# Another order and other gaps for the steps of a chunk recurrence inside a dense matmul stream

## The chip, the cores and the metric

One core of a Trainium2 chip runs one inference step of a two-layer streaming encoder. The metric is device time in microseconds (us); the median of three runs of the kernel before is 3050.2 us (3047.46 to 3052.67). Engines are named as in the profile: PE (TensorE matmuls), PEld (its weight loads), DVE (VectorE), ACT (ScalarE), POOL (GpSimd) and SP (SyncE, whose queue issues the DMAs).

## The reference

Layer one is an RWKV-7 time mixing over 1024 prompt frames and 64 frames of a running stream, then a SwiGLU feed-forward; layer two is sliding-window attention with a shared K/V, then another feed-forward. What matters here is the recurrence, for each of 16 heads with a 64 by 64 state:

```python
def step(s, inp):
    r_t, w_t, k_t, v_t, a_t, b_t = inp
    sa = jnp.einsum('bhvk,bhk->bhv', s, a_t)
    s = s * w_t[:, :, None, :] + sa[..., None] * b_t[:, :, None, :] + v_t[..., None] * k_t[:, :, None, :]
    return s, jnp.einsum('bhvk,bhk->bhv', s, r_t)
```

The feed-forward, which runs beside it, is `(silu(x @ w_gate) * (x @ w_up)) @ w_out` with 2816 hidden units on 1024 features.

## The kernel before, in words

**The recurrence in chunks.** The frames are cut into 17 chunks of 64 (16 of the prompt, one of the running stream). Within a chunk the steps are replaced by matrix products and by the inverse of a 64 by 64 triangular matrix for each head. Chunks 0 to 7 run in one way (`recur_free`), chunks 8 to 16 in another (`recur`), beside the feed-forward of the first half of the prompt ("half A"). Only `recur` is touched by the change.

**The steps of one chunk**, each a Python generator whose `yield`s separate pieces; a piece holds PE work and the DVE, ACT and POOL work that hangs on it:

- `prep` loads r, k, a, s and scales them (elementwise on DVE, ACT, POOL); then the *norms* (16 small matmuls into `p_rp`, read by DVE L187); then two *triangle groups* (8 row pairs of 64x128 matmuls each into `p_rp`, masked into the tile `r_G` by DVE L210); then the *bonus* (one 128x512 product into `p_rp`, DVE L219).
- `inverse16` first works on DVE alone. ACT copies the diagonal blocks out of `r_G` (four copies, L325), DVE transposes them (L330), eliminates (L334 to L359: among them seven pairs of L348 and L351) and turns the result back (L363 to L369). Four *joins* follow, groups of small matmuls into `p_rc`, each of which needs what DVE or ACT made of the join before it: join 1 needs the tile `r_ixd` that DVE L369 wrote; join 2 needs ACT L385; join 3 needs DVE L392 and a second L369; join 4 needs ACT L403 and DVE L404, which copy the result of join 3 out of PSUM. DVE L415 and ACT L414 then write the finished inverse `W`.
- `chain` is the serial part, five pieces: c0 (X times the state, copied out by ACT L435), c1 (times `W`, copied out by DVE L440 and ACT L441 into `r_sv`), c2 (the new state, DVE L447 and L448), c3 and c4 (the output `p_ry`; a one-element POOL memset, L459, stands between its two halves as an ordering point).
- `turned` (called "keys" in `recur`) transposes `r_BK` on PE; `post` normalises the output and, one round later, transposes it.

**A round.** The main loop of `recur` interleaves the chain of chunk i with the joins of chunk i+1 and with `prep` of chunk i+2, and ends by starting the DVE part of the inverse of chunk i+2.

**What sets the order.** From chunk 8 on, PE's order is written by hand. The dense code emits its matmuls in threes of 512 columns (`Dense.mm`, lines L604 to L606: high by high, low by high, high by low part), and after each three it calls `Pump.tick`, which subtracts 0.44 ns per column plus 6 ns from a need. When the need is used up, the pump takes the next piece of `recur`, whose PE instructions are then put at this place of the stream. So a `yield x * us` in `recur` says how much dense matmul time is put on PE before the next piece: a three counts 0.68 us of it. The recurrence's own matmuls are not counted. `FREE` holds the scale, 1.5, and an unscaled gap at the end of a round. PE runs its stream in order: a piece whose inputs are late holds up the dense matmuls behind it. The order on DVE, ACT, POOL and SP is made by the scheduler from priorities and its own estimate of times; there, too, each engine runs in order.

`turns` is the part in which triangle groups (`g`) and joins (`v`) take turns:

```python
for gap in (1.2, 1.4, 1.2, 1.4):
    for x in (g, v):
        if x and next(x, x) is not x:
            yield gap * scale * us
```

The last `next` of `g` ends the generator, and an ended one yields no gap; the order before is therefore triangle 0, join 1, triangle 1, join 2, bonus, join 3, join 4.

Of the kernel before, what the change touches and what calls it, by code (L numbers as in the profile page):

```python
# [499 lines left out]


LOW = 2.5
FREE = (1.5, 5.0)
D, T_P, T_S, NCH = 1024, 1024, 64, 17
NF = 22
RMS_EPS = 1e-5
# [239 lines left out]
def tile_stream_step(ctx: ExitStack, tc: tile.TileContext, I, O):  # L746
# [485 lines left out]
    def recur(chunks, M, base, low, scale, free, ends):  # L1232


        def step(g, p):
            rw.two.at(p, p)
            next(g)
        us = 1000.0
        inv, fill = low + 0.05, low + 0.2
        chunks, ds, gs, vs = list(chunks), [{} for _ in chunks], {}, {}  # L1240

        def load(i, p):
            gs[i] = rw.prep(chunks[i], ds[i])
            step(gs[i], p)

        def inverse(i, p):
            vs[i] = rw.inverse16(ds[i])
            step(vs[i], p)

        def keys(i, p):  # L1250
            rw.two.at(p, p)
            rw.turned(ds[i])

        def turns(g, v, p):

            for gap in (1.2, 1.4, 1.2, 1.4):
                for x in (g, v):
                    if x and next(x, x) is not x:
                        yield gap * scale * us
        load(0, base)  # L1260
        yield 16 * us
        step(gs[0], base)
        yield 4 * us
        rw.two.at(inv, inv)
        yield from turns(gs[0], None, base)
        inverse(0, base)
        keys(0, base)
        load(1, inv)
        yield 12 * us
        step(gs[1], inv)  # L1270
        yield 4 * us
        rw.two.at(inv, inv)
        yield from turns(gs[1], vs[0], inv)
        inverse(1, inv)
        old = None
        for i, ch in enumerate(chunks):
            g, v = None, vs.get(i + 1)
            k = rw.chain(ch, ds[i], M)
            step(k, base)
            yield 1.8 * scale * us  # L1280
            step(k, base)
            if old:
                step(old, fill)
            yield 1.8 * scale * us
            step(k, base)
            M = ds[i]["M"]
            if i + 1 < len(chunks):
                yield scale * us
                keys(i + 1, inv)
            if i + 2 < len(chunks):  # L1290
                load(i + 2, inv)
                g = gs[i + 2]
            yield 2 * scale * us
            step(k, base)
            yield 1.6 * scale * us
            step(k, base)
            if ch in ends:
                M = ends[ch](M)
            old = rw.post(ch, ds[i])
            step(old, fill)  # L1300
            yield 2 * scale * us
            if g:
                step(g, inv)
                yield 2 * scale * us
            rw.two.at(inv, inv)
            yield from turns(g, v, inv)
            if i + 2 < len(chunks):
                inverse(i + 2, inv)
            yield free * us
        step(old, fill)  # L1310
# [12 lines left out]
    def saved(M):  # L1323
# [3 lines left out]
        return M  # L1327

    pump.start(recur(range(8, 17), M, 3, 4, *FREE, {
        15: saved, 16: lambda M: nc.sync.dma_start(O["wkv_s"], M.rearrange("p a b -> p (a b)"))}), 3)  # L1330
    prio(4)
# [361 lines left out]
```

## Time and profile before

| | |
|---|---|
| median of 3 runs | 3050.2 us |
| the profiled execution: its time | 3049.59 us |
| its span, first to last instruction | 3047.8 us |
| PE busy | 2849.6 us (93%) |
| DVE, ACT, POOL busy | 1828.2 (60%), 1342.9 (44%), 911.8 us (30%) |
| mean granted PE clock | 0.96 of full speed |
| `recur` and the dense work beside it | about 700 to 1290 us of the span |

In a row of a group or of the timeline, "L404 DVE COPY r_ixd<-p_rc 32x256" is line 404, its engine, its operation, the tile that it writes and those that it reads (buffer numbers left out); "[2.77 <-DVE r_ixd L404]" says that the engine stood idle for 2.77 us just before, and that the last thing it waited for was that instruction. Idle time counts only on an engine whose order sets the end.

### The profile page before, as it was taken

To read this page: it belongs to the slowest core of one execution; us is meant where nothing else is said; L and a number is where in the kernel's file an instruction comes from. 1 tells how busy PE (TensorE), PEld (TensorE's weight loads), DVE (VectorE), ACT (ScalarE), POOL (GpSimd) and SP (SyncE) were. 2 spreads that over 40 slices of the span, in tenths; PEclk is the share of its full clock that TensorE was granted. 3 is DMA by queue.
4 is the path that set the end of the run, shared out by engine and by line. 5 is a ranking of instruction groups with operands and counts; after the bars stand their busy time and mean duration, and the time that the engine had idled before them with its cause. 6 is when DMAs were issued, how large, how long until landed. Compare 5 with 4: busy or idle time off the path is not lost. (4 is left out here: it accounts for less than half of the span.)

```text
span 3047.8 us, 53525 instructions
## 1 busy us (share of the span) xinstructions
PE 2849.6 (93%) x20802; PEld 2455.3 (81%) x20802; DVE 1828.2 (60%) x3630; ACT 1342.9 (44%) x2485; POOL 911.8 (30%) x795
## 2 busy tenths in 40 slices
PE   6898888978899999999999999999999999999998
PEld 5677677876677777787789999888777888999998
DVE  8887789967777676457654333565554345533334
ACT  7766665544444444334653222344554233322222
POOL 6554134333333333324211222143111222322221
PEclk9999878988999999999999999999999999999999
DMA  4645353344233222352212222222222332322222
GB/s 145 173 121 151 112 139 93 108 121 124 67 94 107 92 84 84 105 143 81 68 49 70 84 81 81 79 82 83 63 67 75 95 93 73 104 84 84 84 84 70
DMA packets 262055, 289.23 MB, mean 95 GB/s; under 512 B 125029, under 2 KB 143973, under 8 KB 261801
## 3 DMA queue, kind: packets, MB, share of 16 engines
q1 hardware_dynamic: 261800, 285.81, 31.6%
q8 instruction: 163, 2.67, 0.4%
q14 instruction: 92, 0.75, 0.1%
HBM read 243.18 MB, written 41.16 MB: 93 GB/s over the span
## 5 line engine op out<-in xcount | busy, mean ns | idle before, releaser
L604 PE MATMUL dp<-xh,wh 128*128 128x288 f32 (+2 forms) x3480 | 1194.8, 344 | 34.6 <-ACT xh L596 15.1
L605 PE MATMUL dp<-xl,wh 128*128 128x288 f32 (+2 forms) x3480 | 1173.4, 337 | 6.7 <-DVE xl L597 5.1
L606 PE MATMUL dp<-xh,wl 128*128 128x288 f32 (+2 forms) x3480 | 1168.5, 336 | 0.0
L564 ACT CAST wh<-wr 128x512 fp32r<-128x512 f32 x730 | 447.0, 619 | 843.5 <-PE dp L605 672.9
L604 PEld LDWEIGHTS dp<-xh,wh 128*128 128x128 f32 x3480 | 669.0, 193 | 115.9 <-ACT xh L596 18.1
L605 PEld LDWEIGHTS dp<-xl,wh 128*128 128x128 f32 x3480 | 669.8, 192 | 69.8 <-DVE xl L597 9.0
L606 PEld LDWEIGHTS dp<-xh,wl 128*128 128x128 f32 x3480 | 669.6, 192 | 57.6 <-issue 2.8
L565 POOL TENSOR_TENSOR wl<-wr,wh 128x512 fp32r<-128x512 f32 x243 | 333.5, 1372 | 1055.1 <-ACT wh L564 965.0
L565 DVE TENSOR_TENSOR wl<-wr,wh 128x512 fp32r<-128x512 f32 x487 | 380.0, 783 | 418.5 <-ACT wh L564 412.3
L604 PE MATMUL dp<-mh,wh 128*128 128x288 f32 (+1 forms) x808 | 255.0, 316 | 4.3 <-DVE hx L1135 2.6
L606 PE MATMUL dp<-mh,wl 128*128 128x288 f32 (+1 forms) x808 | 254.5, 315 | 0.0
L605 PE MATMUL dp<-ml,wh 128*128 128x288 f32 (+1 forms) x808 | 254.0, 314 | 0.0
L1135 DVE TENSOR_TENSOR a_xB<-dp,a_xB 128x288 f32<-128x288 f32 x352 | 158.2, 456 | 85.0 <-PE dp L606 84.6
L1116 DVE TENSOR_TENSOR st<-st,dp 128x288 f32<-128x288 f32 (+1 forms) x132 | 70.2, 532 | 220.9 <-PE dp L606 220.5
L1118 POOL TENSOR_TENSOR xl<-st,xh 128x288 fp32r<-128x288 f32 (+1 forms) x102 | 100.5, 985 | 316.1 <-ACT xh L1117 307.3
L604 PEld LDWEIGHTS dp<-mh,wh 128*128 128x128 f32 x808 | 152.7, 189 | 14.8 <-DVE hx L1135 3.6
L606 PEld LDWEIGHTS dp<-mh,wl 128*128 128x128 f32 x808 | 152.5, 189 | 8.7 <-issue 2.4
L605 PEld LDWEIGHTS dp<-ml,wh 128*128 128x128 f32 x808 | 152.7, 189 | 7.0 <-issue 1.1
L1135 DVE TENSOR_TENSOR hx<-dp,hx 128x512 f32<-128x512 f32 x176 | 119.8, 685 | 45.3 <-PE dp L606 44.1
L1114 ACT ACTIVATE st<-dp 128x288 f32<-128x288 f32 (+1 forms) x132 | 62.1, 470 | 92.5 <-PE dp L606 92.1
L1117 ACT CAST xh<-st 128x288 fp32r<-128x288 f32 (+1 forms) x102 | 50.2, 492 | 110.0 <-DVE st L1116 109.0
L597 POOL TENSOR_TENSOR xl<-st,xh 128x512 fp32r<-128x512 f32 (+2 forms) x37 | 64.7, 1759 | 70.2 <-ACT xh L596 66.2
(378 smaller groups left out, 3839.6 us busy)
## 6 DMA issues: line engine op xcount, KB each, us to landing
wr<-in_ffn_in SPq DMA_DIRECT2D x352, 256.0 KB
wr<-in_ffn_out SPq DMA_DIRECT2D x176, 256.0 KB
wr<-in_rkv SPq DMA_DIRECT2D x90, 256.0 KB
wr<-in_rwo SPq DMA_DIRECT2D x32, 256.0 KB
wr<-in_wq SPq DMA_DIRECT2D x32, 256.0 KB
wr<-in_wo SPq DMA_DIRECT2D x32, 256.0 KB
r_r_s<-s_s SPq DMA_DIRECT2D x17, 256.0 KB
r_sv<-s_vt SPq DMA_DIRECT2D x17, 256.0 KB
```

The lines of the kernel that those rows point to most:

```text
L564: nc.scalar.copy(h, x)
L565: (nc.gpsimd if self.turn % 3 == 0 else nc.vector).tensor_tensor(out=l, in0=x, in1=h, op=ALU.subtract)
L597: (eng or self.nc.vector).tensor_tensor(out=lo, in0=x, in1=hi, op=ALU.subtract)
L604: self.nc.tensor.matmul(ps, lhsT=wh, rhs=xh, start=i == 0, stop=False)
L605: self.nc.tensor.matmul(ps, lhsT=wh, rhs=xl, start=False, stop=False)
L606: self.nc.tensor.matmul(ps, lhsT=wl, rhs=xh, start=False, stop=i == last)
L1114: S.activation(t[o], p, AF.Silu)
L1116: V.tensor_tensor(out=t[o], in0=t[o], in1=p, op=ALU.mult)
L1117: S.copy(a.hi[:, q], t[o])
L1118: G.tensor_tensor(out=a.lo[:, q], in0=t[o], in1=a.hi[:, q], op=ALU.subtract)
L1135: V.tensor_tensor(out=self.x[m][:, q], in0=p, in1=self.x[m][:, q], op=ALU.add)
```

## The change

It changes nothing that is computed and moves only gaps and pieces in `recur`:

- `turns` lists its pieces: join 1, triangle 0, join 2, triangle 1, join 3, bonus, join 4, with gaps of 1.6, 1.6, 1.2, 2.0, 1.6, 3.0 and 0.6 us (times 1.5) behind them. Each join now comes ahead of the piece of `prep` with which it is paired, and the bonus with the longest gap stands between join 3 and join 4.
- In the main loop the gap ahead of c4 grows from 1.6 to 2.4, the two behind `post` and behind the norms shrink from 2 to 1.
- The gap at the end of a round shrinks from 5.0 to 3.0 us (unscaled).

```diff
-FREE = (1.5, 5.0)
+FREE = (1.5, 3.0)
...
         def turns(g, v, p):
 
-            for gap in (1.2, 1.4, 1.2, 1.4):
-                for x in (g, v):
-                    if x and next(x, x) is not x:
-                        yield gap * scale * us
+            for x, gap in ((v, 1.6), (g, 1.6), (v, 1.2), (g, 2.0), (v, 1.6), (g, 3.0), (v, 0.6), (g, 0.0)):
+                if x and next(x, x) is not x:
+                    yield gap * scale * us
...
             yield 2 * scale * us
             step(k, base)
-            yield 1.6 * scale * us
+            yield 2.4 * scale * us
             step(k, base)
             if ch in ends:
                 M = ends[ch](M)
             old = rw.post(ch, ds[i])
             step(old, fill)
-            yield 2 * scale * us
+            yield scale * us
             if g:
                 step(g, inv)
-                yield 2 * scale * us
+                yield scale * us
             rw.two.at(inv, inv)
             yield from turns(g, v, inv)
             if i + 2 < len(chunks):
                 inverse(i + 2, inv)
             yield free * us
```

How the change moves instructions is shown at two places on DVE, in the round around 950 us of the trace before (the one that quoted rows of the timeline come from; `r_f_531` is the work tile of the inverse that starts there, `r_ixd` and `p_rc` the tiles of the joins of the chunk before it). The first place is where DVE copies the result of join 3. Before:

```order
L330 STREAM_TRANSPOSE r_f_531_10217<-r_f_529_10210 128x512
L334 SCALAR_TENSOR_TENSOR r_f_531_10217<-r_f_531_10217,lanes 128x16x16
L343 TENSOR_TENSOR r_f_532_10221<-xl,r_nl_9937 128x128
L335 TENSOR_TENSOR r_f_531_10217<-r_f_531_10217,r_nl_9937 128x16x16
L219 TENSOR_TENSOR r_vf_10126<-p_rp_10128,r_vf_10126 128x512
L168 SCALAR_TENSOR_TENSOR r_rkr_10436<-r_r_a_10417,vecs 128x512
L340 TENSOR_TENSOR r_f_532_10221<-r_f_531_10217 128x128
L169 SCALAR_TENSOR_TENSOR r_rkr_10436<-r_rkr_10436,r_r_k_10416 128x512
L341 TENSOR_TENSOR r_f_531_10217<-r_f_531_10217,r_f_532_10221 128x8x16
L406 COPY r_G_9320<-r_AR_9159 64x8x64
L343 TENSOR_TENSOR r_f_532_10221<-xl,r_nl_9937 128x128
L404 COPY r_ixd_9599<-p_rc_10137 32x256
```

The change:

```order
L394 TENSOR_SCALAR W<-r_ixd_9677,lanes 128x8x32
L210 TENSOR_TENSOR r_G_10067<-p_rp_10150,c_mask 128x512
L210 TENSOR_TENSOR r_G_10067<-p_rp_10151,c_mask 128x512
L565 TENSOR_TENSOR wl_10369<-wr_10370,wh_10368 128x512
L330 STREAM_TRANSPOSE r_f_531_10295<-r_f_529_10288 128x512
L1116 TENSOR_TENSOR st_10089<-st_10089,dp_10103 128x512
L406 COPY r_G_9420<-r_AR_9210 64x8x64
L334 SCALAR_TENSOR_TENSOR r_f_531_10295<-r_f_531_10295,lanes 128x16x16
L343 TENSOR_TENSOR r_f_532_10299<-xl,r_nl_9997 128x128
L404 COPY r_ixd_9677<-p_rc_10177 32x256
```

The copy L404 moved ahead of L335, L219, L168, L340, L169, L341 and the second L343, and the second triangle group's masking (L210) now stands between join 2 (L394) and it.

The second place is where DVE copies the result of c1, in the round two later (around 1090 us). Before:

```order
L367 STREAM_TRANSPOSE r_f_622_11501<-r_f_622_11501 128x256
L368 COPY r_ixd_11525<-r_f_622_11501 128x256
L369 STREAM_TRANSPOSE r_ixd_11525<-r_ixd_11525 128x256
L1116 TENSOR_TENSOR st_11529<-st_11529,dp_11543 128x512
L172 TENSOR_TENSOR r_r_a_11715<-r_r_a_11715,r_rt_11721 128x512
L565 TENSOR_TENSOR wl_11791<-wr_11792,wh_11790 128x512
L1135 TENSOR_TENSOR hx_7492<-dp_11606,hx_7492 128x512
L440 COPY r_sv_11565<-p_rc_11618 64x8x64
```

The change:

```order
L172 TENSOR_TENSOR r_r_a_11776<-r_r_a_11776,r_rt_11782 128x512
L363 TENSOR_SCALAR r_f_622_11586<-r_f_622_11586,lanes 128x8x16
L1135 TENSOR_TENSOR hx_7534<-dp_11666,hx_7534 128x512
L367 STREAM_TRANSPOSE r_f_622_11586<-r_f_622_11586 128x256
L565 TENSOR_TENSOR wl_11905<-wr_11906,wh_11904 128x512
L1135 TENSOR_TENSOR hx_7541<-dp_11674,hx_7541 128x512
L565 TENSOR_TENSOR wl_11911<-wr_11912,wh_11910 128x512
L368 COPY r_ixd_11610<-r_f_622_11586 128x256
L440 COPY r_sv_11642<-p_rc_11681 64x8x64
L496 TENSOR_TENSOR r_g_11253<-p_ry_11185,r_g_11253 128x512
```

L440 still stands behind nearly the whole elimination of the next inverse; in this round the last turn (L369) has moved behind it, and two more rows of dense work (L1135, L565) stand ahead of it.

## The prediction

> **What bounds the kernel now.** I read the page first, then the stretches of time, then PE's idle time by group, then the timeline of one round.
>
> ```profile
> span 3047.8 us, 53525 instructions
> PE 2849.6 (93%) x20802; PEld 2455.3 (81%) x20802; DVE 1828.2 (60%) x3630; ACT 1342.9 (44%) x2485; POOL 911.8 (30%) x795
> ```
>
> PE is the bound. The stretches say where it is not full (columns: stretch, its length, busy us and count of PE, PEld, DVE, ACT, POOL, granted PE clock, DMA share, GB/s):
>
> ```profile
> 665.00:1305.00 640.00, 579.46 (x5488) 448.22 (x5487) 424.29 (x837) 257.32 (x401) 205.09 (x177) 0.94 0.33 99
> 800.00:1212.00 412.00, 382.23 (x3962) 296.69 (x3963) 288.54 (x598) 171.06 (x263) 133.01 (x119) 0.95 0.29 89
> 1700.00:1800.00 100.00, 99.81 (x752) 99.33 (x751) 34.53 (x64) 28.00 (x55) 22.29 (x21) 1.00 0.26 84
> ```
>
> Dense work alone keeps PE at 99.81 of 100 us and full clock. Beside the recurrence PE loses 29.8 of 412 us to waiting and 5% of its clock. A microsecond won on PE there is won at the end, since PE is full afterwards and DMA at about 0.3. What the recurrence's matmuls wait for, over 665 to 1305 us:
>
> ```profile
> L109 PE MATMUL p_rc<-r_ixd 32*32 32x16 f32 (+1 forms) x864 | 16.6, 192 | 25.1 <-DVE r_ixd L404 23.9 <-ACT r_ixd L403 1.1
> L109 PE MATMUL p_ry<-r_M,r_AR 64*64 64x64 f32 x288 | 12.3, 224 | 8.1 <-POOL r_by L459 8.1
> L109 PE MATMUL p_rp<-r_AR,r_BK 64*128 64x128 f32 x288 | 22.5, 295 | 3.2 <-DVE r_n L187 3.2
> ```
>
> So join 4 costs 25.0 us waiting for the copies of join 3 (eight rounds, about 3 each), and the second half of c3/c4 costs 8.1 us behind POOL's memset. One round on PE (step, and how it is fed):
>
> ```profile
> 940.67 1.16 PE L109 MATMUL p_rp<-r_AR,r_BK 64*128 64x128 f32 x16
> 944.05 0.72 PE L109 MATMUL p_rc<-r_ixd 32*32 32x16 f32 x64
> 946.91 1.02 PE L109 MATMUL p_rp<-r_rkr,c_bd 128*128 128x512 f32 x2
> 949.25 0.21 PE L109 MATMUL p_rc<-r_ixd,r_G 32*32 32x32 f32 x1
> 952.16 0.24 PE L109 MATMUL p_rc<-r_ixd 32*32 32x32 f32 x2
> 955.17 1.06 PE L109 MATMUL p_rc<-r_ixd 32*32 32x32 f32 x30 [2.77 <-DVE r_ixd L404]
> 965.76 1.15 PE L109 MATMUL p_rc<-r_sv,r_G 128*64 128x64 f32 x32
> 969.81 1.15 PE L109 MATMUL p_rc<-r_rt,W 64*64 64x64 f32 x32
> 974.25 1.19 PE L109 MATMUL p_rc<-r_sv,r_BT 128*64 128x64 f32 x32
> ```
>
> These are triangle 1, join 2, bonus, join 3, join 4 (its first two matmuls, then the rest 3.0 us later), c0, c1, c2. DVE in the same round, from the start of the next inverse to the copy for join 4:
>
> ```profile
> 948.22 0.71 DVE L330 STREAM_TRANSPOSE r_f<-r_f 128x512 f32<-128x512 f32 x1 [0.62 <-ACT r_f L325]
> ...
> 950.66 0.41 DVE L335 TENSOR_TENSOR r_f<-r_f,r_nl 128x256 f32<-128x256 f32 x1
> 951.00 0.68 DVE L219 TENSOR_TENSOR r_vf<-p_rp,r_vf 128x512 f32<-128x512 f32 x1
> 951.60 0.68 DVE L168 SCALAR_TENSOR_TENSOR r_rkr<-r_r_a,vecs 128x512 f32<-128x512 f32 x1
> 952.20 1.13 DVE L340 TENSOR_TENSOR r_f<-r_f 128x128 f32<-128x128 f32 x1
> 953.25 0.68 DVE L169 SCALAR_TENSOR_TENSOR r_rkr<-r_rkr,r_r_k 128x512 f32<-128x512 f32 x1
> ...
> 954.69 0.43 DVE L404 COPY r_ixd<-p_rc 32x256 f32<-32x256 f32 x1
> ```
>
> Join 3 ended near 950, but its copy L404 came at 954.69: DVE was not idle but busy with other work that stands ahead of it.
>
> The half clock comes from the same stall. Dense matmuls start 0.42 us apart just behind a join 4, 0.24 a little later:
>
> ```profile
> 895.22 1.05 PE L109 MATMUL p_rc<-r_ixd 32*32 32x32 f32 x30 [4.21 <-DVE r_ixd L404]
> ...
> 897.23 0.63 PE L606 MATMUL dp<-xh,wl 128*128 128x512 f32 x1
> 897.65 0.63 PE L604 MATMUL dp<-xh,wh 128*128 128x512 f32 x1
> ...
> 900.16 0.39 PE L604 MATMUL dp<-xh,wh 128*128 128x512 f32 x1
> 900.40 0.39 PE L605 MATMUL dp<-xl,wh 128*128 128x512 f32 x1
> ```
>
> **The change part by part.** It adds and removes no work; outside the recurrence every engine's order is as before. The gaps of a round sum to 12.2 x 1.5 + 9.0 x 1.5 + 5.0 = 36.8 us before and 11.0 x 1.5 + 11.6 x 1.5 + 3.0 = 36.9 after, so the same dense work passes in a round, and all that can change is waiting.
>
> *Join 4.* A dense matmul takes 0.233 us start to start. From triangle 1 to join 4 the change has 42 dense matmuls (9.8 us) and three steps that each add a little: triangle 1 and 9 matmuls took 944.05 - 940.67 = 3.38, so 1.3; join 3 and 9 took 2.91, so 0.8; the bonus and 6 took 2.34, so 0.9. Join 4 is reached 12.8 us after triangle 1. DVE starts L330 7.5 us after triangle 1 here (948.22 - 940.67), as it waits for ACT's four copies, and less in other rounds; one round earlier triangle 1 was at 879.33:
>
> ```profile
> 885.72 0.71 DVE L330 STREAM_TRANSPOSE r_f<-r_f 128x512 f32<-128x512 f32 x1 [2.92 <-ACT r_f L325]
> ```
>
> That is 6.4; I take 6.7. From L330 to the end of L404 the order now has 2.3 to 4.2 us of work, without the 4 us of L335, L219, L168, L340, L169 and its neighbours. L404 ends 9.0 to 10.9 us after triangle 1: two to four microseconds early. I take all 25.0 us as gained (bound: 15, if every round kept 1.2).
>
> *The clock.* Behind the stall that ended at 895.22 nine matmuls ran at 0.19 us extra, and the join itself was slower (1.05 us against 0.73 below); rounded, 2.0 us, eight times 16 (from the window's 0.95: at most 0.05 x 412 = 21; at least 10).
>
> ```profile
> 1196.53 0.73 PE L109 MATMUL p_rc<-r_ixd 32*32 32x32 f32 x30 [2.26 <-DVE r_ixd L404]
> 1196.50:1198.50 2.00, 1.97 (x33) 1.71 (x34) 1.93 (x6) 0.98 (x2) 0.52 (x2) 0.64 0.00 0
> ```
>
> The shortest of the stalls, 2.26 us, already has the clock down (0.64 in the two microseconds behind it). [...]
>
> *POOL's memset.* Between c2 and c4 the dense count grows from 30 to 36, 1.4 us. The waits were 8.1 us in five rounds, 2.3 at most; with 1.4 off each, about 1.5 stay: 6.6 gained (0 to 8.1, if POOL's chain from the keys through L170, L176, L177 moves along).
>
> *What is late next: c2.* The stalls also gave DVE time to catch up. c2 needs `r_sv`, written by DVE L440 and, behind it, ACT L441; L440 stands behind the whole elimination. Groups over 800 to 1212 us:
>
> ```profile
> L348 DVE TENSOR_TENSOR r_f<-r_f,r_f 128x28 f32<-128x28 f32 (+3 forms) x49 | 14.9, 305 | 1.4
> L351 DVE TENSOR_REDUCE r_f<-r_f 128x14 f32<-128x42 f32 (+3 forms) x49 | 11.6, 237 | 1.4
> L565 DVE TENSOR_TENSOR wl<-wr,wh 128x512 fp32r<-128x512 f32 x61 | 47.2, 775 | 17.8 <-ACT wh L564 16.0 <-PE p_rp L113 1.3
> L1135 DVE TENSOR_TENSOR hx<-dp,hx 128x512 f32<-128x512 f32 x63 | 42.7, 682 | 7.0 <-PE dp L606 6.4
> L440 DVE COPY r_sv<-p_rc 64x512 f32<-64x512 f32 x7 | 4.8, 682 | 7.7 <-PE p_rc L109 7.7
> L441 ACT COPY r_sv<-p_rc 64x512 f32<-64x512 f32 x7 | 4.1, 585 | 1.6 <-DVE r_sv L440 1.4
> ```
>
> Before, DVE waited 7.7 us in seven rounds at L440, 1.1 each, while PE lost 3 to the stall and 2 to its clock: without these DVE would be the late one. From triangle 1 to c2 PE now needs 84 dense matmuls (19.5 us) and, for triangle 1, join 3, bonus, join 4 (0.8), c0 (4.05 - 2.79 = 1.3) and c1 with the transpose (974.25 - 969.81 - 2.79 = 1.65), 6.8: 26.3 us. DVE needs 6.7, then its rows from L330 through L440, then 0.6 for L441. These rows are 34 to 37 of the recurrence (about 15.5 us: seven L348 and L351 make 3.8, L440 0.7, the rest the other named steps by their means in the same view) and the dense rows that the new order puts among them (three to five L565, none to eight L1135, up to two others). Round by round that sums to 18.9, 18.9, 19.7, 21.0, 21.9, 24.7, 22.2 and 20.4 us. The first round has only 72 dense matmuls (23.1 us), the fourth 87 (27.0). So c2 is late by 3.1, 0, 0.7, 1.3, 2.9, 5.7, 3.2 and 1.4: 18 us. Four stalls above 2.2 us bring the half clock back, 8 us. Bounds: the same sums for the rounds before came out between 3.3 us under and 0.8 over what the timeline shows, so 1.5 either way a round: 8 to 30 for the stalls, 2 to 16 for the clock.
>
> *Costing nothing.* Join 1 comes earlier, but its tile is ready by c2 and it is wanted over 15 us later. The second triangle group of the first rounds waited 3.2 us for L187; at that place a norm of the dense work waits for the same DVE queue, so I count nothing (3.2 either way). The recurrence's loads and the weight loads share SP's queue; they keep their distances in dense work, at a DMA share of 0.29.
>
> Sum: 25.0 + 16 + 6.6 - 18 - 8 = 21.6 us gained. The profiled execution took 3049.59 us (span plus 1.8), 0.6 under the median; 3049.6 - 21.6 = 3028.
>
> **The rivals.** *A, the stall only vanishes:* DVE is not late at c2, since dense rows fall elsewhere than the order suggests. For it: the 1.1 us that DVE had over. Against: the sums above. 47.6 gained: 3002.
>
> *B, slower: the copies ahead of L330 are late.* L330 now follows the masking directly, and everything on DVE, evacuations of dense results included, queues behind it while ACT, with its weight casts in front, makes four copies:
>
> ```profile
> L325 ACT COPY r_f<-r_G 32x512 f32<-32x512 f32 x28 | 30.8, 1101 | 5.7 <-DVE r_G L210 5.4
> L330 DVE STREAM_TRANSPOSE r_f<-r_f 128x512 f32<-128x512 f32 x7 | 5.0, 711 | 22.5 <-ACT r_f L325 22.5
> ```
>
> Those are 4.4 us a round, and DVE idled 3.2 for them. If casts in between made it 5 us later, c2 would be late by about 7 in each of eight rounds (57 us) at half clock behind each (16): 73 against 47.6, or 3075. It turns slower from about 3 us a round. Against: ACT was held 5.4 us in all here, by DVE.
>
> *C, little changes at join 4:* L404 stays behind L330 and is late by 1 us or so, enough to keep the clock down; then 15 + 4 + 6.6 - 12 come out, 3036, or nothing with c2 as estimated.
>
> *D, the clock hangs on long gaps only:* if only stalls as long as the 4.21 us of the row at 895.22 brought it down (two before, with the first round's 3.63; one after), the old ones' clock was worth 4 and the new ones' 2: 25 + 4 + 6.6 - 18 - 2 = 15.6, 3034. The row at 1196.50 speaks against it.
>
> **How the numbers follow.** Forecast 0.50, A 0.22, B 0.09, C 0.14, D 0.05. The time is the forecast's, 3028; its own range is 3015 to 3040. The range for all, 3004 to 3045, takes in most of A, C and D and leaves out B and the best of A. A measurement here tells about 0.2%, 6 us. Forecast, A, D and most of C are faster by more: 0.87. The rest of C and the mild part of B are within: 0.07. Slower, B: 0.06.
>
> **What would show it.** Right: join 4's wait for L404 under 5 us in all; c2's matmuls (into `p_rc` from `r_sv`, `r_BT`) waiting for L440 or L441, longest in the round near 1090 us; the memset's wait under 3; the clock near 0.97 beside the recurrence. Wrong: no wait at c2 (A); L330 idle well over 3.2 us a round and dense matmuls waiting for L1135 (B); L404 still on top (C). A dense stream waiting for weights would break the whole sum.

## The result, and the profile after

The changed kernel takes 3028.8 us (median of four runs, 3027.2 to 3032.0) against 3049.0 (3047.5 to 3052.7) for the one before: a ratio of 0.9933, 95% interval 0.9916 to 0.995. The forecast was 3028.

The page of the changed kernel:

```profile
span 3025.4 us, 53491 instructions
PE 2837.6 (94%) x20802; PEld 2443.9 (81%) x20802; DVE 1835.6 (61%) x3630; ACT 1344.4 (44%) x2485; POOL 916.4 (30%) x795
```

To compare kernels, the same piece of the program is cut out of each: from the DVE product L496 that starts at 672.8 us before to the DVE sum L1071 that starts at 1337.3. In the change these start at 676.1 and 1316.0. The stretches view of before, and then of after (columns as before: stretch, length, busy us of PE, PEld, DVE, ACT, POOL, granted PE clock, DMA share, GB/s):

```profile
672.80:1337.30 664.50, 602.24 (x5594) 467.81 (x5595) 446.63 (x869) 270.82 (x422) 206.38 (x178) 0.94 0.34 102
```

```profile
676.10:1316.00 639.90, 588.91 (x5594) 455.31 (x5595) 450.79 (x869) 272.16 (x422) 208.85 (x178) 0.96 0.36 106
800.00:1212.00 412.00, 393.91 (x4113) 304.57 (x4114) 304.53 (x613) 180.86 (x277) 141.47 (x124) 0.98 0.32 95
```

The counts agree, so the work is the same, and it takes 24.6 us less: PE is idle for 51.0 us instead of 62.3 (length less busy time), 11.3 less, and busy for 13.3 us less at the same count of matmuls, which is half clock that is gone: the granted clock was 0.94 before and is 0.96 after. In the table of experiments below, "idle" and "busy" are meant in this way. The spans differ by 22.4: before this stretch the execution of the change lost 3.3 us (676.1 against 672.8), behind it it won 1.1, in places where the order is the same.

What PE waited for in that stretch, in the waits view of before and of after (us in total, times, longest):

```profile
PE p_rc L109 <- DVE r_ixd L404: 23.9, 8, 4.2
PE p_ry L109 <- POOL r_by L459: 8.1, 5, 2.3
PE dp L705 <- DVE lo L697: 4.1, 2, 2.5
PE dp L604 <- DVE hx L1135: 3.7, 3, 1.8
PE p_rp L109 <- DVE r_n L187: 3.2, 1, 3.2
```

```profile
PE dp L604 <- DVE hx L1135: 8.9, 7, 3.5
PE dp L705 <- DVE lo L697: 8.0, 2, 7.2
PE p_ry L109 <- POOL r_by L459: 3.6, 3, 1.7
PE p_ry L113 <- POOL r_yc L491: 3.4, 1, 3.4
PE p_rc L109 <- ACT r_rt L435: 3.1, 1, 3.1
PE p_rc L109 <- ACT r_sv L441: 3.1, 4, 2.2
PE p_rc L109 <- DVE r_sv L440: 2.9, 4, 1.4
```

Join 4 waits for nothing any more. In its place stand waits of the chain's c2 (L440, L441) and c1 (L435), of dense matmuls for DVE's sums (L1135), of a dense norm (L705) and of the last transposes (L491). The round near 950 us on PE after the change:

```profile
936.82 1.16 PE L109 MATMUL p_rp<-r_AR,r_BK 64*128 64x128 f32 x16
940.88 0.73 PE L109 MATMUL p_rc<-r_ixd 32*32 32x16 f32 x64
943.12 1.16 PE L109 MATMUL p_rp<-r_AR,r_BK 64*128 64x128 f32 x16
950.70 1.02 PE L109 MATMUL p_rp<-r_rkr,c_bd 128*128 128x512 f32 x2
956.53 0.69 PE L109 MATMUL p_rc<-r_ixd 32*32 32x32 f32 x32
968.75 1.97 PE L109 MATMUL p_rc<-r_rt,W 64*64 64x64 f32 x32 [3.12 <-ACT r_rt L435]
```

These are triangle 0, join 2, triangle 1, the bonus, join 4 (now in one piece of 32 matmuls) and c1. DVE in the same round:

```profile
950.02 0.71 DVE L330 STREAM_TRANSPOSE r_f<-r_f 128x512 f32<-128x512 f32 x1 [3.64 <-ACT r_f L325]
...
952.19 0.47 DVE L334 SCALAR_TENSOR_TENSOR r_f<-r_f,lanes 128x256 f32<-128x256 f32 x1
952.59 0.27 DVE L343 TENSOR_TENSOR r_f<-xl,r_nl 128x128 f32<-128x128 f32 x1
952.89 0.43 DVE L404 COPY r_ixd<-p_rc 32x256 f32<-32x256 f32 x1
```

L404 ends 3.2 us before join 4 wants it; L334 and L343 are there for a comparison further down. And why c1 was held at 968.75, in ACT's timeline:

```profile
967.59 0.62 ACT L1117 CAST xh<-st 128x512 fp32r<-128x512 f32 x1 [4.54 <-DVE st L1116]
968.11 0.58 ACT L435 COPY r_rt<-p_rc 128x512 f32<-128x512 f32 x1
```

ACT's copy of c0 stood behind a dense cast, and that cast stood idle for 4.5 us for a DVE sum (L1116) which stands on DVE, busy without a gap, behind the elimination (L1116 started at 966.87, PE had nothing left to do from 965.63). So DVE's lateness came to PE by way of ACT's queue, 4.5 us at the cast and 3.1 at c1: c1 is a victim of DVE although it does not read anything that DVE wrote late.

### The profile page after: what moved, and what is told of

It is laid out like the page before. It is cut to its first block, busy times and chain, and to the rows that moved or that the text cites. A ratio compares the mean times of both kernels' runs of the same rounds, so it can differ in the third digit from the quotient of the medians.

```text
span 3025.4 us, 53491 instructions
## 1 busy us (share of the span) xinstructions
PE 2837.6 (94%) x20802; PEld 2443.9 (81%) x20802; DVE 1835.6 (61%) x3630; ACT 1344.4 (44%) x2485; POOL 916.4 (30%) x795
## 5 line engine op out<-in xcount | busy, mean ns | idle before, releaser
L565 POOL TENSOR_TENSOR wl<-wr,wh 128x512 fp32r<-128x512 f32 x243 | 336.5, 1385 | 1036.2 <-ACT wh L564 944.9
L565 DVE TENSOR_TENSOR wl<-wr,wh 128x512 fp32r<-128x512 f32 x487 | 377.6, 778 | 422.6 <-ACT wh L564 416.4
L1135 DVE TENSOR_TENSOR a_xB<-dp,a_xB 128x288 f32<-128x288 f32 x352 | 158.1, 456 | 85.2 <-PE dp L606 84.8
L1118 POOL TENSOR_TENSOR xl<-st,xh 128x288 fp32r<-128x288 f32 (+1 forms) x102 | 100.6, 986 | 332.3 <-ACT xh L1117 320.0
L1116 DVE TENSOR_TENSOR st<-st,dp 128x288 f32<-128x288 f32 (+1 forms) x132 | 70.1, 531 | 203.7 <-PE dp L606 203.2
L1135 DVE TENSOR_TENSOR hx<-dp,hx 128x512 f32<-128x512 f32 x176 | 119.5, 685 | 42.1 <-PE dp L606 41.2
```

The source lines that it names most:

```text
L565: (nc.gpsimd if self.turn % 3 == 0 else nc.vector).tensor_tensor(out=l, in0=x, in1=h, op=ALU.subtract)
L1116: V.tensor_tensor(out=t[o], in0=t[o], in1=p, op=ALU.mult)
L1118: G.tensor_tensor(out=a.lo[:, q], in0=t[o], in1=a.hi[:, q], op=ALU.subtract)
L1135: V.tensor_tensor(out=self.x[m][:, q], in0=p, in1=self.x[m][:, q], op=ALU.add)
```

## The experiments

Medians of four runs are given with the range (that of before and of the change stands above), single runs without. All kernels ran beside the kernel before, which took 3049 to 3052 us in each group. The stretch is the one defined above, in one profiled execution of each kernel.

| kernel | time, us | stretch | PE busy | PE idle |
|---|---|---|---|---|
| before | 3049.0 | 664.5 | 602.2 | 62.3 |
| the change | 3028.8 | 639.9 | 588.9 | 51.0 |
| new gaps in the chain and at the end, old turns | 3058.8 | 670.0 | 602.6 | 67.4 |
| change, long gap behind join 4 | 3029.3 | 640.2 | 591.3 | 48.9 |
| change, less elimination on DVE | 3018.0 | 631.0 | 586.7 | 44.3 |
| change, triangles ahead of joins | 3017.5 (3014.1 to 3021.0) | 634.9 | 585.8 | 49.1 |
| before, join 3 and bonus exchanged | 3026.3 (3023.5 to 3027.1) | 641.3 | 589.9 | 51.4 |
| triangles ahead, last transposes covered | 3021.3 | 633.9 | 586.7 | 47.2 |
| the same, longer gap ahead of join 3 | 3010.6 (3007.6 to 3012.9) | 626.5 | 586.7 | 39.8 |
| change, casts on DVE | 3008.0 (3006.6 to 3010.2) | 627.0 | 586.5 | 40.5 |
| before, casts on DVE | 3035.3 (3031.2 to 3038.3) | 649.4 | 595.1 | 54.3 |
| best: longer gap ahead of join 3, casts on DVE | 2997.4 (2993.9 to 3001.1) | 614.2 | 584.8 | 29.4 |

### The gaps without the turns

The changed kernel with the old order and gaps in `turns`; only the chain's gaps and the one at a round's end stay new.

```diff
-            for x, gap in ((v, 1.6), (g, 1.6), (v, 1.2), (g, 2.0), (v, 1.6), (g, 3.0), (v, 0.6), (g, 0.0)):
-                if x and next(x, x) is not x:
-                    yield gap * scale * us
+            for gap in (1.2, 1.4, 1.2, 1.4):
+                for x in (g, v):
+                    if x and next(x, x) is not x:
+                        yield gap * scale * us
```

> The changed kernel with the old order and gaps among triangle groups and joins (join 3 and join 4 again 1.8 us apart); the shorter gap at the round's end, the longer one ahead of c4 and the shorter ones behind post and norms are kept. Theory (the gain is join 4's stall and the clock behind it): join 4 waits for L404 again, 20 to 28 us in the region, eight or nine times; the half clock comes back behind each; a round is 3.9 us of dense work shorter, so DVE is later still: 3045 to 3060. Rival (the gain comes from the gaps at the round's end and ahead of c4): the time stays within 6 us of the changed kernel's 3029.

Measured: 3058.8 us, 7 above the kernel before beside it (3051.9). Its waits view:

```profile
PE p_rc L109 <- DVE r_ixd L404: 29.2, 8, 4.8
```

The shorter round leaves DVE less time for the copies of join 3, and join 4 waits 5.3 us more than before. So there is no gain without the new `turns`. The longer gap ahead of c4 does do its part: the memset's waits are 2.3 us here, against 8.1 before.

### The long gap moved behind join 4

```diff
-(v, 1.6), (g, 3.0), (v, 0.6)
+(v, 1.6), (g, 0.6), (v, 3.0)
```

> The changed kernel with its order, but the 3.0 gap that stands ahead of join 4 put behind it (0.6 ahead, 3.0 behind); the sum of a round is the same. Join 4 is then reached 3.6 us earlier, some 9.2 us behind triangle 1, where L404 ends 9 to 11 us behind it. Theory (the gap ahead of join 4 is what removes the stall; the order of the pairs does the rest): join 4 waits 0 to 2 us a round, 5 to 12 in all, c2 is as late as in the changed kernel less what PE lost at join 4; time 3028 to 3040. Rival (the order of the pairs alone removes the stall): no wait at join 4 and 3029.

Measured: 3029.3 us, the change's time, as the rival has it. Join 4 waits for L404 by 2.3 us in four rounds (1.0 the longest) and once for L403 (0.7) instead of not at all. So the gap of 3.0 units (4.5 us) ahead of join 4, the part of the edit that looks made for it, is hardly needed: the bonus and 3.3 us of gaps between joins 3 and 4 nearly do, where the kernel before had 1.8 us and no bonus. Whether a longer gap there without the bonus would do the same was not run.

### Less work in the elimination

Four of the seven L348 and L351 pairs are left out of every inverse, so the inverse is not the full one.

```diff
-        for j in range(14, 0, -2):
+        for j in range(14, 8, -2):
```

> The changed kernel with four of the seven elimination steps on DVE (pairs of L348 and L351) left out in the 16-wide inverse, so the inverse is not computed in full; everything else is done. About 2.2 us of DVE work a round less between triangle 1 and c2. Theory (the waits at c1, c2 and of dense matmuls for L1135 and L1116, 16.8 us in the changed kernel, are all DVE being late): they fall to 2 to 7 us and the two or three half-clock stretches behind them go, time 3010 to 3020. Rival (they come from ACT's queue or from the weight casts, not from DVE's load): they stay over 12 us and the time within 6 us of 3029.

Measured: 3018.0 us. DVE's busy time in the stretch falls from 450.8 to 436.3, PE's idle time from 51.0 to 44.3. Not all waits answer: those of c2 fall from 6.0 to 3.3 and the memset's from 3.6 to 1.7, but the dense matmuls' for L1135 stay (8.9 and 9.0, the longest 3.5 in both), and so nearly does c1's for L435 (3.1 and 2.5). The waits that were to fall from 16.8 us to between 2 and 7 are some 14 still, which is the rival's side, while the time is in the theory's range. The theory that the elimination is what makes DVE late is half right at best; something else holds L1135 up. The casts on DVE, below, show a part of it.

### Triangles ahead of the joins again

The changed kernel with the joins no longer leading in the first two pairs; the order is then triangle 0, join 1, triangle 1, join 2, join 3, bonus, join 4.

```diff
-            for x, gap in ((v, 1.6), (g, 1.6), (v, 1.2), (g, 2.0), (v, 1.6), (g, 3.0), (v, 0.6), (g, 0.0)):
+            for x, gap in ((g, 1.6), (v, 1.6), (g, 1.2), (v, 2.0), (v, 1.6), (g, 3.0), (v, 0.6), (g, 0.0)):
```

> The changed kernel with its gaps at their places, but the triangle group ahead of the join in the first two pairs, as before the change. Theory (the gap between join 3 and join 4 is what counts; the order within a pair decides only what stands between the second triangle group and join 3): the second triangle group is 2.4 us earlier against join 4, so L330, L404 and L440 are all earlier: no wait at join 4, c2 less late; 5 to 10 us faster than the changed kernel, 3019 to 3025. Rival (joins leading is what removes the stall): join 4 waits again, over 10 us, and the time is 3037 or more.

Measured: 3017.5 us, ratio to before 0.989 (0.9871 to 0.9908), 11 us faster than the change and a little under the range expected. Of the 11, 5.0 lie in the stretch; the rest lies ahead of it (2.9) and behind (3.2), where the order is the same in both, and is not explained. So the part of the change that its description puts first, the joins' lead over the triangles, gains nothing and seems to cost some 5 us: with it c1 and the readers of L1135 wait, without it the waits are less in sum and stand elsewhere, at join 3 (L369) and at the dense norm (L705, 10.7). DVE ahead of join 3 in this kernel:

```profile
996.72 0.71 DVE L330 STREAM_TRANSPOSE r_f<-r_f 128x512 f32<-128x512 f32 x1 [2.22 <-ACT r_f L325]
997.36 0.25 DVE L392 TENSOR_TENSOR r_ixd<-p_rc,r_ixd 128x128 f32<-128x128 f32 x1
997.53 1.43 DVE L334 SCALAR_TENSOR_TENSOR r_f<-r_f,lanes 128x256 f32<-128x256 f32 x1
998.88 1.35 DVE L343 TENSOR_TENSOR r_f<-xl,r_nl 128x128 f32<-128x128 f32 x1
1000.15 0.43 DVE L369 STREAM_TRANSPOSE r_ixd<-r_ixd 128x256 f32<-128x256 f32 x1
```

Join 2 was done by 994.4 (PE 993.71 + 0.73), but its sum L392 stood behind L330, which waited 2.22 us for ACT's copies; behind it came two instructions that took 1.43 and 1.35 us, where the rows of the change have 0.47 and 0.27 for the same lines; POOL was at work beside both (casts at 997.41 and 998.64, more of that below). Join 3 waited 3.3 us here, 10.6 in five rounds. This is rival B's mechanism, at a place that the prediction had not thought of.

### Only join 3 and the bonus exchanged

The kernel before, no gap changed.

```diff
-            for gap in (1.2, 1.4, 1.2, 1.4):
-                for x in (g, v):
-                    if x and next(x, x) is not x:
-                        yield gap * scale * us
+            for x, gap in ((g, 1.2), (v, 1.2), (g, 1.4), (v, 1.4), (v, 1.2), (g, 1.2), (v, 1.4), (g, 0.0)):
+                if x and next(x, x) is not x:
+                    yield gap * scale * us
```

> The kernel before with one thing changed: in each pair of turns the order stays triangle 0, join 1, triangle 1, join 2, but join 3 now stands ahead of the bonus instead of behind it; no gap is changed (1.2, 1.2, 1.4, 1.4, 1.2, 1.2, 1.4 times 1.5, the gaps of the chain and at the round's end as before). Theory (the gain comes from the bonus and its gap standing between join 3 and join 4, and the joins that lead the triangles cost time): join 4 gets 2.7 us more, so its waits fall from 25 us to between 2 and 8, the half clock behind them goes in most rounds, the memset's waits (8.1 us) stay; some of the lateness comes back at join 3, which has 2.7 us less behind join 2: 3 to 8 us there. Time 3024 to 3034. Rival (the whole change is needed: the joins' lead gives the copies their time): join 4 keeps over 12 us of waits, and the time is 3040 or more.

Measured: 3026.3 us, ratio to before 0.9916 (0.99 to 0.9933): this exchange alone does as much as the whole change. Join 4 has no wait left; the largest ones in the rounds are those of join 3 and of the memset:

```profile
PE p_rc L109 <- DVE r_ixd L369: 16.3, 8, 3.1
PE p_ry L109 <- POOL r_by L459: 7.6, 5, 2.2
```

The waits for L369 came out at twice the 3 to 8 us expected, those of join 4 at none instead of 2 to 8. The same 2.7 us, taken from behind join 2 and put ahead of join 4, shift the wait by one join. Its idle time is that of the change (51.4 and 51.0).

### The last transposes covered, and more time ahead of join 3

First, one gap of 4 us ahead of the last piece of the recurrence, on top of the order with triangles ahead; then, beside it, 2.1 us a round moved from ahead of join 4 to ahead of join 3.

```diff
             yield free * us
+        yield 4 * us
         step(old, fill)
```

```diff
-(v, 2.0), (v, 1.6), (g, 3.0), (v, 0.6)
+(v, 3.4), (v, 1.6), (g, 1.6), (v, 0.6)
```

> The run with the triangle groups ahead of the joins (3017.5 us), plus one gap of 4 us of dense work ahead of the last transposes of the recurrence, where POOL's L491 was waited for by 3.35 us. Theory (PE is full behind the recurrence, so a wait that is covered there is won at the end): that wait is 0, 3.4 us fewer of PE idle time, and the half clock of 6.8 us behind it (3.4 us lost) goes as well: 3.4 to 6.8 us less, 3010 to 3014. Rival (dense matmuls behind the recurrence wait for something else that now comes later): the wait moves to the dense matmuls behind, 3016 to 3019.

> The kernel of the run before this one (triangles ahead of the joins, the late last transposes covered), with 2.1 us of dense work moved in each round from ahead of join 4 to ahead of join 3 (gap behind join 2 from 2.0 to 3.4, gap behind the bonus from 3.0 to 1.6, times 1.5). Theory (each wait belongs to its own copy, and join 4 has more than it needs since the bonus stands ahead of it): join 3's waits for L369 fall from 10.6 us (five, 3.3 at most) to under 3, join 4 waits under 3, two episodes of half clock go: 3002 to 3008. Rival (DVE as a whole is late, so that the wait only moves along the round as it did with the change): join 3's gain comes back at join 4, c1, c2 or at dense evacuations, and the time is within 3 us of the run before this one.

Measured: the cover removes the wait for L491 (3.4 to 0), but the norm waits grow from 10.7 to 12.4 and L1135's from 3.1 to 3.5: 1.0 us is won in the stretch, and the one run, 3021.3, lies at the upper end of what the kernel without the cover took (3014.1 to 3021.0). The expectation of 3.4 us or more failed. The longer gap ahead of join 3 gives 3010.6 us, ratio to before 0.9868 (0.9853 to 0.9882), between the ranges of theory and rival, and 7.4 us less in the stretch. L369 is not among the waits any more and join 4 waits for nothing, as the theory has it. But of the 10.7 us, 7.2 came back, as the rival has it: at dense matmuls for L1135 (3.5 to 6.2) and L1116 (2.5), at the memset (1.3) and at c1 for L415 (0.7). c2 won 0.9, and another 3.2 came outside the rounds: ahead of the first one the norm's wait at L705 shrank from 9.9 to 2.2 while the triangles' for L187 grew from 0 to 5.6, and behind the last one L705 waited 1.4 instead of 2.5. So here dense work moved to a wait won about a third of it; the rest is DVE's lateness, which finds another reader.

### POOL's casts given to DVE

While the recurrence is fed, the weight casts that POOL makes, every third L565, go to DVE. PE's order is untouched.

```diff
-        (nc.gpsimd if self.turn % 3 == 0 else nc.vector).tensor_tensor(out=l, in0=x, in1=h, op=ALU.subtract)
+        (nc.gpsimd if self.turn % 3 == 0 and not (self.pump and self.pump.gen) else nc.vector).tensor_tensor(out=l, in0=x, in1=h, op=ALU.subtract)
```

> The changed kernel, with the weight casts that POOL makes (every third L565) given to DVE as long as the recurrence is being fed, 44 of them; PE's order is the same. In the trace of the change, DVE instructions that read two inputs from SBUF take about 0.85 us longer than their like when a POOL instruction overlaps them (245 of 1055 that overlap one, none of 2575 that don't); between 788 and 1260 us that is 42 us of DVE's time, 16.7 of it beside POOL's L565. Theory (DVE is held while POOL reads): DVE gets 38 casts of 0.69 us more there, 26 us, but its excess falls from 42 to 22 to 27 us, so its busy time grows by under 12 us, and the waits of PE for DVE (16.8 us) grow by less than 6; time 3024 to 3034. Rival (the long instructions are long for another reason, the overlap is chance): the excess stays near 40 us, DVE has 26 us more to do, PE waits 10 us or more longer, 3038 or more.

The stretch of this kernel, the same work with 41 more DVE instructions in it (910 against 869):

```profile
674.30:1299.60 625.30, 586.13 (x5594) 453.91 (x5595) 456.63 (x910) 271.38 (x422) 155.07 (x136) 0.96 0.35 109
```

DVE's busy time grows by 5.8 us only (450.8 to 456.6) for 41 instructions that take 0.69 each, 28 us; POOL's falls by 53.8. Instructions of DVE that took over 0.25 us more than their like numbered 71 in the change from 665 us to the end of the stretch, and cost 55.5 us; here they are 47 and cost 36.4. The excess fell and the busy time grew by under 12 us, both as the theory has it. Its time did not hold: 3009.5 us instead of 3024 to 3034. Most of PE's waits for DVE or POOL fell: L1135 from 8.9 to 5.2, c2 from 6.0 to 4.4, c1 for L435 from 3.1 to 1.7, the memset from 3.6 to 0.5. The norm's (L705) stayed at 8.0, and small ones grew (L1118 from 0.3 to 1.6, L415 from 0.3 to 0.8). The memset's wait is POOL's own queue, so not all of the gain is DVE's. The same kernel timed:

> The changed kernel with the casts on DVE once more, for an interval: the one look gave 3009.5 us. Theory (the gain of 14.6 us in the stretch of the recurrence is real: 10.2 us less waiting, 1.7 us less half clock): 3008 to 3016. Rival (the one look was a lucky execution): 3020 or more.

Measured: 3008.0 us, ratio 0.9863 (0.9848 to 0.9877). Its profiled execution, the one in the table, has the same waits within 0.9 us each (L1135 5.9). And on the kernel before, where PE's order is the old one:

> The kernel before with only the casts moved from POOL to DVE while the recurrence is fed; PE's order is unchanged. Theory (join 4's wait in the kernel before is DVE's order, L404 behind L335, L219, L168, L340 and L169, and only partly the held instructions): join 4's waits fall from 25 to between 12 and 22 us, the memset's 8.1 us to under 5 since POOL has 50 us less to do, the half clock behind join 4 mostly stays: 5 to 15 us faster, 3035 to 3045. Rival (the held DVE instructions are what makes the copies late): join 4 under 10 us and 3030 or less.

Measured: 3035.3 us, ratio 0.9951 (0.9935 to 0.9966). Its waits view:

```profile
PE p_rc L109 <- DVE r_ixd L404: 20.6, 8, 3.7
PE p_ry L109 <- POOL r_by L459: 5.2, 5, 1.5
```

Join 4's stall is mostly DVE's order, as the prediction read it, not the held instructions: 20.6 of 23.9 us are left. The memset's 5.2 are a little over the 5 expected, and join 3's wait for L369 grew from 0.8 to 4.3. In the stretch this run wins 8.0 us of idle and 7.1 of busy time.

### Both together

The longer gap ahead of join 3 (with triangles ahead and the last transposes covered) and the casts on DVE.

> The fastest order so far (triangles ahead of the joins, join 3 ahead of the bonus, longer gap ahead of join 3, last transposes covered; 3010.6 us) together with the casts given to DVE while the recurrence is fed. Theory (both take lateness off the same DVE queue, so they overlap: the waits of PE for DVE that are left in that order, about 8 us, and POOL's 1 us, go by half or more, and the half clock behind two of them): 4 to 9 us less, 3002 to 3007. Rival (what was won by the casts on the changed kernel was the same waits that the better order has already removed, and DVE has 7 us more to do): 3009 or more.

Measured: 2997.4 us, ratio to before 0.9827 (0.9809 to 0.9845); 13 us under the better order alone where 4 to 9 were expected. Its stretch, and its waits there:

```profile
673.20:1287.40 614.20, 584.81 (x5594) 453.32 (x5595) 452.04 (x911) 271.79 (x422) 159.51 (x135) 0.97 0.37 111
```

```profile
PE dp L604 <- ACT xh L596: 11.4, 2, 9.3
PE dp L705 <- DVE lo L697: 5.8, 2, 3.3
PE dp L604 <- DVE hx L1135: 4.3, 5, 1.8
```

What is left of PE's idle time stands mostly ahead of the rounds: of 29.4 us, some 19 lie before 756 us (most of the 9.3 of one wait for L596 that ends at 681, 3.3 for L705 at 746), some 5 behind 1260, and 4.3 in the rounds between.

## Why the prediction was right, point by point

**Join 4: right, place and size.** 25.0 us were taken as gained, and 25.0 are gone. The working held as well: L330 started 6.4 to 7.1 us behind triangle 1 (6.7 taken; 6.9 in the round shown, 950.02 less 943.12), join 4 came 13.4 us behind it there (12.8 taken, with 42 dense matmuls between them; the trace has 45), and L404 ended 2.8 to 3.9 us ahead of join 4 in the eight rounds (two to four). What the prediction did not see is which edit did it: the exchange of join 3 and the bonus, alone, removes all of it.

**The clock: the price of a stall too low, the balance 5 us short.** 16 less 8 were forecast: 2.0 us for each of eight old stalls and of four new ones. Between 775 and 1212 us the records of the granted clock show half speed for 44.4 us before, in eight stretches, one at each stall of join 4, and for 17.1 after, in three (at 801, 968 and 1135 us, at the waits for L441, L435 and L1135): 22 us of clock before and 8.5 after, 2.8 us a stall in both. The 8 for the new ones came out right because one stall fewer met a higher price. The bound of 21 was read off a window that starts at 800, behind the first of the eight stretches (777 to 784). PE's busy time at the same work fell by 13.3 us, 5 more than the balance of 8.

**POOL's memset: a little less.** 8.1 to 3.6: 4.5 gained, 6.6 forecast, inside its bounds.

**What is late next: the sum right, the place only in part.** 18 us of DVE's lateness were forecast, all at c2, longest near 1090 us. In the stretch it came out as 6.0 at c2 (L440, L441), 3.4 at c1 (L435 3.1, L415 0.3) and 5.9 more at dense matmuls (L1135 from 3.7 to 8.9, L1116 0.7): 15.3. Taken by rounds, with every reader of DVE's lateness between triangle 1 and c2 counted, the waits over 0.25 us sum to 3.9, 1.0, 0.3, 3.1, 2.1, 2.3, 3.5 and 0.4, against 3.1, 0, 0.7, 1.3, 2.9, 5.7, 3.2 and 1.4 forecast. The largest miss is the round near 1090, named as the longest: c2 waited about 1 us there (0.68 for L440), dense matmuls ahead of it 1.3 for the same queue (1075 and 1082), and 3.4 of the 5.7 did not come at all; the cause of that is not known. The fourth round, where 1.8 came on top at c1, makes up for half of it in the sum. The step that failed is the one that let c2 alone meet DVE's lateness: other readers of DVE's results, and what stood behind them, met 9.3 of the 15.3 us, and in rounds four, five, seven and eight a reader ahead of c2 took the whole wait.

**Costing nothing: right as a sum.** The triangles' wait for L187 (3.2), the keys' (1.0) and join 3's (0.8) went, and the norm of the dense work, named as the danger there, waits longer (L705, 4.1 to 8.0).

**Missed: the end.** The last transposes wait 3.4 us for L491, because the shorter gaps behind `post` and at a round's end leave less dense work ahead of them: with these gaps and the old turns they wait 4.5 us, with the old gaps and join 3 exchanged with the bonus not at all. The prediction counted dense work per round and did not look at the last one.

**The rivals.** A (no lateness anywhere) is out by the 15.3 us. B did not happen in the change: DVE's idle time ahead of L330 fell over 800 to 1212 us:

```profile
L330 DVE STREAM_TRANSPOSE r_f<-r_f 128x512 f32<-128x512 f32 x7 | 5.0, 712 | 18.2 <-ACT r_f L325 18.2
```

It was 22.5 us. One of B's signs did come, weakly: dense matmuls wait 8.9 us for L1135 instead of 3.7. C (L404 still late) is out. D (only long stalls cost clock) is out: all eight stalls of 2.3 to 4.2 us had a stretch of half clock, and 13.3 us of busy time went with them.

So the mechanism was right in its main terms, and that the forecast of 21.6 us met 22.4 in the spans so closely is luck: errors of a few us each cancelled: clock +5.3, lateness +2.7, memset -2.1, the end -3.4, outside the stretch -2.2, and small ones +0.4 in all.

## What to carry to other kernels

In these runs a wait that was removed at one reader came back in good part at others in the stream: of 10.7 us at join 3, 7.2 stood elsewhere with the longer gap, and the exchange that took 25.0 us from join 4 put 16.3 at join 3, where 0.8 had been. So price the lateness of a queue as a sum, and don't trust its place. Cut such an edit into its parts before believing in any of them; here one exchange alone gained as much as the whole edit, and the part named first seems to have cost time. And before reordering around an engine that is late, look for instructions of it that take longer than their like, and at what runs beside them; in the change 71 such instructions of DVE cost it 55.5 us beside the recurrence.

## What the runs showed of the hardware

**Some DVE instructions took longer while POOL worked.** Here are two groups of DVE instructions of the same size, by line over the whole span of the change (ns: shortest/median/longest):

```profile
L565 DVE TENSOR_TENSOR wl<-wr,wh x487: 647/692/1954, 40.4 to 2988.8; 128x512 fp32r<-128x512 f32 x163
```

```profile
L1135 DVE TENSOR_TENSOR hx<-dp,hx x176: 648/685/693, 818.6 to 2583.8; 128x512 f32<-128x512 f32 x176
```

L565 reads two tiles from SBUF, L1135 one from PSUM and one from SBUF. Of these 487 L565, 161 overlap a POOL instruction, and 54 of the 161 take over 1 us; of the 326 others none takes over 0.70. None of the 56 L1135 of the second row that overlap one takes over 0.70. Over all DVE instructions of that trace, 245 took over 0.4 us more than the median of their form, 216 us in all; each of them overlapped a POOL instruction (by over 30 ns), as did only 810 of the 3385 others. Of the 245, 244 started behind the POOL instruction beside them, and all ended within their own usual length after it. 32 of them are copies and TENSOR_SCALARs with one tile of data, so the two inputs that the expectation names are not the whole condition; none reads or writes the PSUM tiles `dp`, `p_rc`, `p_rp` or `p_ry`. Two such rows, and POOL beside them:

```profile
1131.12 1.54 DVE L565 TENSOR_TENSOR wl<-wr,wh 128x512 fp32r<-128x512 f32 x1
1132.59 1.53 DVE L169 SCALAR_TENSOR_TENSOR r_rkr<-r_rkr,r_r_k 128x512 f32<-128x512 f32 x1
```

```profile
1131.08 1.04 POOL L479 TENSOR_TENSOR r_vf<-r_vf,vecs 128x512 f32<-128x512 f32 x1 [1.44 <-DVE r_vf L219]
1132.22 1.35 POOL L151 TENSOR_TENSOR r_rt<-r_r_k,vecs 128x512 f32<-128x512 f32 x1
```

These two cost DVE some 1.7 us just ahead of the sum L1135 for which dense matmuls waited 3.5 us at 1134.8, the wait that a shorter elimination did not move and that the casts on DVE shortened to 2.0 and 2.8 in two executions. The run with the casts on DVE shows the price: POOL's busy time fell by 53.8 us and DVE's grew by 5.8. Why DVE's instructions took longer is not shown.

**Whether a stall of 1.5 to 3.5 us cost clock varied.** Over the 13 profiled executions, between 765 and 1300 us, each stall of PE with no other over 0.25 us within 8 us of it was held against the records of the granted clock: half clock began within some 4 us of its end for 1 of some 60 stalls under 1.5 us, 3 of 19 up to 2, 9 of 16 up to 2.5, and 25 of 27 longer ones. The same stall of 3.4 us at the last transposes brought half clock in five executions (of four kernels) and none in the change, where a stretch behind it stands beside one behind the 3.5 us stall:

```profile
1134.80:1141.00 6.20, 6.20 (x28) 4.70 (x30) 5.51 (x16) 1.24 (x2) 0.00 (x0) 0.72 0.15 51
1260.00:1266.00 6.00, 6.00 (x29) 4.95 (x28) 2.08 (x3) 1.74 (x3) 1.44 (x2) 1.00 0.31 101
```

In the trace of before two stalls of the same length differ, one of 2.27 us that ended at 986.54 and one of 2.26 that ended at 1196.50:

```profile
987.00:993.00 6.00, 6.00 (x72) 4.90 (x68) 4.62 (x9) 2.36 (x4) 1.41 (x1) 1.00 0.27 65
1196.50:1200.50 4.00, 3.97 (x38) 3.23 (x39) 3.54 (x10) 0.98 (x2) 1.51 (x2) 0.57 0.23 66
```

Of the 160 stretches at half clock behind 700 us, 134 last 3.4 us or twice that (25 of the 29 in before and the change). What decides whether a stall brings one is not shown. The prediction was right to go by its row at 1196.50, but a fixed price per stall, 2.0 us as it used it, is not what the runs show either.
